# A hybrid decoder block on one core: one weight piece asked for and rounded a step later, retention's tables held in their place, and two probability turns one piece later

## Chip, cores, metric

One core of one Trainium2 chip. The metric is the device time of one execution in microseconds, the median of the runs. Engines: PE (TensorE), DVE (VectorE), ACT (ScalarE), POOL (GpSimd) and SP, which here only issues DMAs.

## The reference

One decoder layer for 1024 rows of width 1024, in float32. What matters here is the part for differential attention:

```
h    = rms_norm(x, norm1_g)
proj = h @ w_in                                  # [1024, 1024] @ [1024, 3584], columns split among the head groups
ret  = rms_norm(retention(rotary(rq), rotary(rk), rv)) * silu(rg)      # 8 heads, chunks of 128 rows
q_d, k_d = rms_norm(dq), rms_norm(dk)            # 4 heads, two score maps each
a    = softmax(q1 k1^T / 8) - lam * softmax(q2 k2^T / 8)               # causal
dif  = rms_norm(a @ v) * (1 - lambda_init)
x    = x + concat([ret, dif]) @ w_out
x    = x + (silu(rms_norm(x) @ w_gate) * (rms_norm(x) @ w_up)) @ w_down
```

## The kernel before, in words

**Products in three parts.** Every large product is done with operands split into a high and a low half (`whi`, `wlo`, and `act` for the rows): three matmuls hi·hi, hi·lo, lo·hi (`mm3`). A weight piece is loaded by SP into `raw`, ACT rounds it (`whi`), DVE takes the rest (`wlo`).

**Steps.** The input projection is done in steps `s` (the loop near L978). Step `s` computes one tile of 128 rows for one column group: eight pieces `k` = 0..7, each one `mm3`. Groups 0 to 3 are the four heads of differential attention (32 steps, 384 columns each), groups 4 to 7 are pairs of retention heads (512 columns). `run` (L509) issues piece `k` and then every operation that is listed for that `k`. Operations of differential attention come from the table `DIF_PLAN` (L76): an entry is (lag, k, function, argument); in step `s` the function works on unit `s - lag`. Unit `u` is row tile `t = u % 8` of head `u // 8`, and its scores have `t + 1` blocks of 128 columns. So a step works on four units at once: it prepares the queries of unit `s-1`, does scores and exponentials of unit `s-2`, and turns and multiplies the probabilities of unit `s-3`.

**The names that follow.** In the order of one step before the change:
- after k = 2 and k = 3 the scores of the two maps (`d_scores`, PE writes `big`); DVE masks them and takes the maximum (`nm`), ACT takes the exponential (`p<-big,nm`);
- after k = 3 the **turn** (`d_turn`, L760): up to four blocks of probabilities of unit `s-3` are transposed by PE (`m<-cs,p`), and after them blocks 4 to 7 in a second turn; after k = 4 ACT **copies** the first four out of PSUM (`d_take`, `aT<-m`), after k = 5 DVE the others;
- after k = 6 the **query turn** (`d_qkturn`, `m<-cs,qkn`) of unit `s-1`, and behind it the **values** product of unit `s-3` (`m<-v,aT`);
- then ACT writes `q` and `kh`, DVE their low halves `q`, `kl` and two casts into `kh`, then the weights `p<-p,by` of unit `s-2`; DVE sums squares of the next unit (`ss`), POOL makes `ms` and `rs` of it, and DVE multiplies (`qkn`), which is what the next query turn reads.

In the first steps the rows of `x` are brought in as well: loaded by SP (`x_load`, `p<-in_x`), transposed by PE in two halves (`x_turn`, **input turn**, also `m<-cs,p`), cast by ACT and subtracted by DVE (`x_split`, `act<-m`), and squared by ACT for the mean (`x_mean`, **square**, `sqx<-p`). Input turns, turns, query turns and values share two PSUM banks (`m`), each free again when its last reader is done.

**Group 1's weight.** `ready` (L954) says in which step each piece of the next group is rounded: piece `k` of group `g` in step `8(g-1) + k`, by `w_part`, once after k = 5 (ACT) and once after k = 6 (DVE). `w_load` asks for the pieces of step `s+1` at the start of step `s`, into two buffers `raw` (NRAW = 2).

**Order.** With `Pinned` (L369) compute operations of the steps keep the order in which the program issues them; others are placed by the scheduler. `r_tables` (L804), three DVE operations that make retention's tables from the row means `ms`, is called at step 32 and is not pinned. `small_loads` (L615) loads gains and lambdas in step 0; `gains` (L627) scales them on DVE in step 1.

Of the kernel before, what the change touches and what calls it, by code (L numbers as in the profile page):

```python
# [20 lines left out]
KC = D // P  # L21
# [31 lines left out]
def constants():  # L53
# [20 lines left out]


DIF_PLAN = [  # L76
    (3, 3, "d_turn", 0),
    (3, 4, "d_take", 0),
    (2, 3, "d_scores", 1),
    (-3, 3, "x_load"),  # L80
    (2, 2, "d_scores", 0),
    (1, 1, "d_sq"),
    (3, 3, "d_turn", 4),
    (-2, 3, "x_turn", 1),
    (3, 5, "d_take", 4),
    (2, 3, "d_max", 0),
# [31 lines left out]
W_PLAN = (5, 6)  # L118
# [245 lines left out]
def block_kernel(ctx: ExitStack, tc: tile.TileContext, x, norm1_g, w_in, ret_norm_g, dq_g, dk_g,  # L364
                 lq1, lk1, lq2, lk2, subln_g, w_out, norm2_g, w_gate, w_up, w_down, cst, out):
    nc = tc.nc
    order = {"pinned": False}
# [131 lines left out]
    def proj(g, t):  # L499

        width = 384 if g < NDH else 512
        pr = prs[g, t] = bankp()
        h = hT[t // 2][:, t % 2]
        for k in range(KC):
            wh, wl = W[g][k]
            mm3(pr[:, :width], h[:, 0, k, :], h[:, 1, k, :], wh, wl, k == 0, k == KC - 1)
            yield

    def run(ops, main):  # L509

        order["pinned"] = main is not None
        for k in range(KC):
            if main is not None:
                next(main)
            for at, f, *args in ops:
                if at == k:
                    f(*args)
        order["pinned"] = False

    def place(plan, names, s, n):  # L520

        return [(at, names[f], s - lag, *args) for lag, at, f, *args in plan if 0 <= s - lag < n]
# [281 lines left out]
    def r_tables():  # L804
        V.reciprocal(rms, ms)
        for dst, at, by in ((vdec, C_VDEC, rms), (eps2, C_EPS, ms)):
            V.tensor_tensor(out=dst, in0=cs[:, at:at + NRH].unsqueeze(1).broadcast_to([P, NT, NRH]),
                            in1=by.unsqueeze(2).broadcast_to([P, NT, NRH]), op=ALU.mult)
# [120 lines left out]
    def o_proj(t, dh):  # L929
        pr = prs["o", t, dh] = bankp()  # L930
        m_ = mT[t // 2][:, t % 2]
        for k in range(KC):
            wh, wl = W[NG + dh][k]
            mm3(pr, m_[:, 0, k, :], m_[:, 1, k, :], wh, wl, k == 0, k == KC - 1)
            yield
# [19 lines left out]
    for g in range(1, NG + 1):  # L955
        for k in range(KC):
            s = (g - 1) * NT + k
            if g == NDH + 1:
                s = max(s, (g - 1) * NT + 4 + k // 2)
            ready.setdefault(s, []).append((g, k, "wp" if g % 2 == 0 else "wd" if g < NDH else "wr"))  # L960
# [17 lines left out]
    for s in range(ND + NR + 3):  # L978
        if s == ND:
            difw.close()  # L980
            rp = ret.enter_context(tc.tile_pool(name="ret", bufs=2, side="right"))
            rg_t = [rp.tile([P, P], F32, name=f"rg{i}", bufs=1) for i in range(2)]
            for i in range(2):
                G.memset(rg_t[i], 0.0)
            qbd_t = [rp.tile([P, 2, P], F32, name=f"qbd{i}", bufs=1) for i in range(2)]
            for qbd in qbd_t:
                G.memset(qbd, 0.0)
            r_tables()
        if s == ND + 2:
            difps.close()  # L990
            rps = retps.enter_context(tc.tile_pool(name="retps", bufs=1, space=bass.MemoryType.PSUM))
        if s == ND + 3:
            dif.close()
            rowb = ctx.enter_context(tc.tile_pool(name="rowb", bufs=NT))
            mixr = [rowb.tile([P, 512], F32, tag="rowb", name="rowb") for _ in range(NT)]
            pools["wr"] = ctx.enter_context(tc.tile_pool(name="wr", bufs=1))
            xp = rets.enter_context(tc.tile_pool(name="xp", bufs=6))
        ops = place(DIF_PLAN, names, s, ND) + place(RET_PLAN, names, s - ND, NR)
        if s == 0:
            ops = [(at, start, what) for at, what in BEGIN] + [op for op in ops if op[1] not in (x_turn, x_split)]  # L1000
            ops += [(7, small_loads)]
        elif s == 1:
            ops += [(5, gains), (7, lambdas)]
            ops += [(at, f, 2, *args) for at, f, *args in LATE]
        ops += [(0, w_load, s + 1)] + [(k, w_part, s) for k in W_PLAN]
        t = s - ND - NR
        if t >= 0:
            ops += [(0, o_load, t, 0), (KC - 1, o_add, t, 0)]
        if s == ND + NR + 2:
            ops += [(3, o_load, 0, 1)]  # L1010
        run(sorted(ops, key=lambda op: op[0]), proj(*divmod(s, NT)) if t < 0 else o_proj(t, 0))
# [299 lines left out]
    for f0 in range(0, NF, 2):  # L1311
        g = Strassen(w_gate, f0, rowb, "rowb").whole() if f0 else firsts[0].out
# [83 lines left out]
```

## Time and profile before

| | |
|---|---|
| median of 3 runs | 1221.82 us (1220.80 to 1221.99) |
| the profiled execution | 1223.85 us, of which the instructions span 1222.0 us |
| PE busy | 1205.5 us, 99% of the span |
| DVE, POOL, ACT busy | 834.7, 571.1, 536.7 us |
| steps of differential attention | about 1.4 to 258 us of the span |

The span runs from the first to the last instruction; 1.85 us of the execution lie around it. PE's busy time is that of matmuls whose ends are modelled, so that a short wait of PE shows less idle time in a row than it costs; the distance between two starts tells more.

### The profile page before, as it was taken

To read this page: it belongs to the slowest core of one execution; us is meant where nothing else is said; L and a number is where in the kernel's file an instruction comes from. 1 tells how busy PE (TensorE), PEld (TensorE's weight loads), DVE (VectorE), ACT (ScalarE), POOL (GpSimd) and SP (SyncE) were. 2 spreads that over 40 slices of the span, in tenths; PEclk is the share of its full clock that TensorE was granted. 3 is DMA by queue.
4 is the path that set the end of the run, shared out by engine and by line. 5 is a ranking of instruction groups with operands and counts; after the bars stand their busy time and mean duration, and the time that the engine had idled before them with its cause. 6 is when DMAs were issued, how large, how long until landed. Compare 5 with 4: busy or idle time off the path is not lost.

```text
span 1222.0 us, 17360 instructions
## 1 busy us (share of the span) xinstructions
PE 1205.5 (99%) x5968; PEld 1024.6 (84%) x5968; DVE 834.7 (68%) x1491; ACT 536.7 (44%) x1194; POOL 571.1 (47%) x719
## 2 busy tenths in 40 slices
PE   8999999999999999999999999999999999999998
PEld 6899989888888888788888888888888888888887
DVE  5988888864444445546988656666566659698697
ACT  6866666653222224334534343333433334444442
POOL 2655555544444443102256456544565436154053
PEclk9999999999999999999899999999999999999999
DMA  6201011103111110422223333323333268943332
GB/s 201 63 26 33 27 29 35 36 10 104 44 44 35 44 35 27 164 87 80 76 87 117 107 106 120 106 87 101 111 114 112 68 226 283 366 142 96 95 117 82
DMA packets 97383, 117.34 MB, mean 96 GB/s; under 512 B 8976, under 2 KB 60304, under 8 KB 97296
## 3 DMA queue, kind: packets, MB, share of 16 engines
q1 hardware_dynamic: 95968, 115.65, 29.4%
q8 instruction: 47, 0.77, 0.3%
q10 hardware_dynamic: 1328, 0.60, 0.2%
q14 instruction: 40, 0.33, 0.1%
HBM read 87.64 MB, written 28.57 MB: 95 GB/s over the span
## 4 chain that ended last, share of the span: by engine, by line
PE 93%; DVE 3%; DMA 2%; issue 1%; ACT 1%; POOL 0%; SPq 0%; ACTq 0%; DVEq 0%; POOLq 0%
PE pp L377 43%; PE h L377 27%; PE m L377 18%; PE big L377 3%; PE o L377 2%; PE it L377 1%; DMA wide<-in_w_down_dram 1%; DMA raw<-in_w_in_dram 1%; DVE act L377 0%; DMA x2d<-x 0%; DVE wlo L377 0%; DVE q L377 0%; DVE x L377 0%; SPq L1295 0%; DVE acc L377 0%
## 5 line engine op out<-in xcount | busy, mean ns | idle before, releaser
L377 PE MATMUL pp<-whi,act 128*128 128x384 f32 (+1 forms) x896 | 287.5, 373 | 0.8 <-ACT whi L377 0.8
L377 POOL TENSOR_TENSOR sum<-rawp 128x512 f32<-128x512 f32 x110 | 157.6, 1434 | 175.5 <-DVE wlo L377 166.4
L377 ACT CAST whi<-sum 128x512 fp32r<-128x512 f32 x165 | 102.6, 622 | 208.0 <-POOL sum L377 66.5
L377 DVE TENSOR_TENSOR wlo<-sum,whi 128x512 fp32r<-128x512 f32 x165 | 165.0, 1001 | 38.6 <-ACT whi L377 38.3
L377 PE MATMUL h<-act,whi 128*128 128x512 f32 x608 | 189.0, 392 | 0.0
L377 PEld LDWEIGHTS pp<-whi,act 128*128 128x128 f32 x896 | 167.3, 189 | 15.3 <-ACT whi L377 1.0
L377 PE MATMUL pp<-wlo,act 128*128 128x384 f32 (+1 forms) x448 | 161.6, 361 | 0.6 <-DVE wlo L377 0.6
L377 POOL TENSOR_TENSOR sum<-wide 128x512 f32<-128x512 f32 x55 | 86.0, 1564 | 129.0 <-DVE wlo L377 111.6
L377 PEld LDWEIGHTS h<-act,whi 128*128 128x128 f32 x608 | 115.2, 190 | 24.0
L377 PE MATMUL pp<-wrh,act 128*128 128x512 f32 x384 | 131.1, 402 | 0.0
L377 PE MATMUL h<-act,wlo 128*128 128x512 f32 x304 | 119.2, 392 | 0.0
L377 PE MATMUL m<-act,whi 128*128 128x512 f32 (+2 forms) x320 | 98.3, 388 | 2.2 <-DVE act L377 2.2
L377 DVE TENSOR_TENSOR wlo<-wide,whi 128x512 fp32r<-128x512 f32 x99 | 77.8, 809 | 32.3 <-ACT whi L377 32.3
L377 PE MATMUL pp<-act,whi 128*128 128x512 f32 (+2 forms) x320 | 98.1, 388 | 0.0
L377 ACT CAST whi<-wide 128x512 fp32r<-128x512 f32 x99 | 59.3, 621 | 83.0 <-PE m L377 43.2
L377 PEld LDWEIGHTS pp<-wlo,act 128*128 128x128 f32 x448 | 85.0, 190 | 7.7 <-DVE wlo L377 1.2
L377 PEld LDWEIGHTS pp<-wrh,act 128*128 128x128 f32 x384 | 72.2, 188 | 14.4
L377 POOL TENSOR_TENSOR fsum<-c 128x512 f32<-128x512 f32 x55 | 78.5, 1438 | 9.9 <-DMA ffd<-fsum 9.9
L377 DVE TENSOR_TENSOR c<-c,h 128x512 f32<-128x512 f32 x86 | 56.8, 682 | 31.2 <-PE h L377 31.1
L377 DVE TENSOR_TENSOR wlo<-rawp,whi 128x512 fp32r<-128x512 f32 x44 | 47.1, 1073 | 40.8 <-ACT whi L377 40.0
L377 PE MATMUL pp<-wrl,act 128*128 128x512 f32 x192 | 74.8, 390 | 0.0
L377 PEld LDWEIGHTS m<-act,whi 128*128 128x128 f32 x320 | 60.5, 191 | 14.2 <-DVE act L377 2.4
(162 smaller groups left out, 2520.6 us busy)
## 6 DMA issues: line engine op xcount, KB each, us to landing
wide<-ffd SPq DMA_DIRECT2D x77, 256.0 KB, 2.7
ffd<-fsum SPq DMA_DIRECT2D x55, 256.0 KB, 2.0
rawp<-in_w_gate_dram SPq DMA_DIRECT2D x22, 512.0 KB, 3.8
rawp<-in_w_up_dram SPq DMA_DIRECT2D x22, 512.0 KB, 3.8
wide<-in_w_down_dram SPq DMA_DIRECT2D x44, 256.0 KB, 5.4
raw<-in_w_in_dram SPq DMA_DIRECT2D x32, 256.0 KB, 2.8
ffd<-c SPq DMA_DIRECT2D x22, 256.0 KB, 2.0
raw<-in_w_in_dram SPq DMA_DIRECT2D x26, 192.0 KB, 2.5
```

Source lines behind the costliest of these rows:

```text
L377: i = getattr(self.engine, op)(*args, **kw)
```

## The change

1. Piece 0 of group 1 is rounded in step 1 in place of step 0, beside piece 1. Both are asked for at the start of step 0. The load of the next piece, which was asked for at the start of step 1, is asked for after k = 7 of that step.
2. `r_tables` is pinned, so its three DVE operations stay at step 32.
3. Both turns (`d_turn` 0 and 4) come after k = 4 in place of k = 3.

```diff
 DIF_PLAN = [
-    (3, 3, "d_turn", 0),
+    (3, 4, "d_turn", 0),
     (3, 4, "d_take", 0),
     (2, 3, "d_scores", 1),
...
     (1, 1, "d_sq"),
-    (3, 3, "d_turn", 4),
+    (3, 4, "d_turn", 4),
     (-2, 3, "x_turn", 1),
...
             s = (g - 1) * NT + k
+            if g == 1:
+                s = max(s, 1)
...
+            order["pinned"] = True
             r_tables()
+            order["pinned"] = False
...
-        ops += [(0, w_load, s + 1)] + [(k, w_part, s) for k in W_PLAN]
+        ops += [(KC - 1 if s == 1 else 0, w_load, s + 1)] + [(k, w_part, s) for k in W_PLAN]
```

On ACT in steps 0 and 1, where `act<-m` are input casts, `whi<-raw` the rounding of a piece of group 1 and `sqx` a square (rows with - are those before, with + those of the change):

```order
 L377 CAST act<-m 128x512
 L377 ACTIVATE sqx,ss<-p 128x1024
-L377 CAST act<-m 128x512
-L377 ACTIVATE whi<-raw,g1col 128x384
-L377 CAST act<-m 128x512
+L377 CAST act<-m 128x512 x2
 L377 ACTIVATE sq<-pp 128x256
 L377 ACTIVATE v<-pp,rs 128x128
```

The rounding that stood between two input casts of step 0 is gone from there; it stands in step 1 ahead of `q`, as the first of two. On SP the third piece of group 1 goes behind the loads of row tiles 4 and 5.

On PE in the step whose probabilities have five blocks (`big` are the two maps' scores, `m<-cs,p` the turns), before and then in the change:

```order
L377 MATMUL big<-kh,q 128x512
L377 MATMUL big<-kl,qz_186 128x512
L377 MATMUL big<-kh,q 128x256
L377 MATMUL big<-kl,qz_186 128x256
L377 MATMUL pp<-whi,act 128x384
L377 MATMUL pp<-wlo,act 128x384
L377 MATMUL pp<-whi,act 128x384
L377 MATMUL m<-cs,p 128x128 x4
L377 MATMUL big<-kh,q 128x512
```

```order
L377 MATMUL big<-kh,q 128x512
L377 MATMUL big<-kl,qz_186 128x512
L377 MATMUL big<-kh,q 128x256
L377 MATMUL big<-kl,qz_186 128x256
L377 MATMUL pp<-whi,act 128x384
L377 MATMUL pp<-wlo,act 128x384
L377 MATMUL pp<-whi,act 128x384
L377 MATMUL m<-cs,p 128x128 x5
L377 MATMUL pp<-whi,act 128x384
```

Before, the first turn stood ahead of the second map's scores and the second turn behind them. Now the scores follow piece 3 at once, piece 4 follows them, and both turns stand together between piece 4 and piece 5.

On ACT in step 3, with what each instruction waits for (`sqx` is the square, `aT` the copy, `act<-m` the input cast, `p<-big` the first exponential), before and then in the change:

```order
L377 ACTIVATE sqx,ss<-p 128x1024 [waits DMAHW5_49,PE_49]
L377 COPY aT<-m 128x128
L377 CAST act<-m 128x512 [waits PE_49]
L377 ACTIVATE p,ls<-big,nm 128x256 [waits DVE_49,Activation_49]
L377 ACTIVATE whi<-raw,g1col 128x384 [waits DMAHW6_49]
```

```order
L377 ACTIVATE sqx,ss<-p 128x1024 [waits PE_49]
L377 COPY aT<-m 128x128
L377 CAST act<-m 128x512
L377 ACTIVATE p,ls<-big,nm 128x256 [waits DVE_49,Activation_49]
L377 ACTIVATE whi<-raw,g1col 128x384 [waits DMAHW6_49]
```

The order on ACT is the same. The copy has no wait of its own in either: the square's wait for PE covers the turn. In the change the input cast has none either, since its input turn now comes ahead of the turn on PE.

## Rows read from the trace of the kernel before

**Rows 1.** The page's first part: busy time of each engine, its share of the span and its instructions.

```profile
PE 1205.5 (99%) x5968; PEld 1024.6 (84%) x5968; DVE 834.7 (68%) x1491; ACT 536.7 (44%) x1194; POOL 571.1 (47%) x719
```

**Rows 2.** Stretches of the span: from and to, length, then busy time of PE, PEld, DVE, ACT, POOL with instructions, the granted clock of PE, the DMA share and GB/s. The first holds steps 0 to 2, the second the eight steps of head 1.

```profile
14.00:32.00 18.00, 15.20 (x88) 13.97 (x87) 11.70 (x32) 11.69 (x31) 7.08 (x17) 0.91 0.42 126
83.00:141.00 58.00, 57.50 (x364) 53.62 (x364) 48.84 (x125) 35.74 (x105) 32.11 (x64) 1.00 0.10 28
```

**Rows 3.** Instructions of ACT in order of time at the end of step 0: start, length, operation, and in brackets the idle time before and what ended it.

```profile
14.35 0.57 ACT L377 CAST act<-m 128x512 fp32r<-128x512 f32 x1
16.27 0.61 ACT L377 ACTIVATE whi<-raw,g1col 128x384 fp32r<-128x384 f32 x1 [1.36 <-DMA raw<-in_w_in_dram]
16.79 0.57 ACT L377 CAST act<-m 128x512 fp32r<-128x512 f32 x1
```

**Rows 4.** Instructions of PE in order of time in steps 1 and 2: three input turns, the query turn of step 1, the first input turn of step 2, the query turn of step 2.

```profile
14.32 0.60 PE L377 MATMUL m<-cs,p 128*128 128x128 f32 x4
...
15.69 0.55 PE L377 MATMUL m<-cs,p 128*128 128x128 f32 x3 [0.25 <-DVE act L377]
...
18.19 0.66 PE L377 MATMUL m<-cs,p 128*128 128x128 f32 x4 [1.85 <-DVE act L377]
...
23.32 0.38 PE L377 MATMUL m<-cs,qkn 128*128 128x128 f32 x2
...
25.13 0.38 PE L377 MATMUL m<-cs,p 128*128 128x128 f32 x2
...
30.02 0.41 PE L377 MATMUL m<-cs,qkn 128*128 128x128 f32 x2 [0.71 <-DVE qkn L377]
```

**Rows 5.** Two stretches, columns as in rows 2.

```profile
18.20:22.50 4.30, 4.30 (x19) 4.20 (x20) 2.37 (x5) 2.88 (x6) 2.29 (x5) 0.60 0.58 160
500.00:520.00 20.00, 18.60 (x95) 15.29 (x94) 9.37 (x15) 7.50 (x18) 2.19 (x7) 1.00 0.53 177
```

**Rows 6.** Step 1: three instructions of DVE in order of time; the issue of the last small load by SP and, from the view of the tile gout, the time from issue to landing of its two loads; the issue of row tile 4 and, from the view of the tile p for this load alone, its time to landing.

```profile
22.73 0.21 DVE L377 TENSOR_SCALAR gout<-gout 128x4 f32<-128x4 f32 x2
22.86 0.61 DVE L377 SCALAR_TENSOR_TENSOR wlo<-raw,g1col,whi 128x384 fp32r<-128x384 f32 x1
24.61 0.35 DVE L377 SCALAR_TENSOR_TENSOR q<-m,gq,q 64x128 fp32r<-64x128 f32 x1 [1.14 <-ACT kh L377]
...
17.68 0.50 SPq L622 DMA_DIRECT2D gout<-in_diff_subln_g_dram  x1
DMA to landing us min/median/max: 4.0/4.2/4.3
...
18.77 0.43 SPq L536 DMA_DIRECT2D p<-in_x_dram  x1
DMA to landing us min/median/max: 4.7/4.7/4.7
```

**Rows 7.** Step 3 in order of time, engine by engine: PE's turn, query turn and values; ACT's square, input cast and q; DVE's subtraction for that input cast; and the square of step 4.

```profile
34.14 0.30 PE L377 MATMUL m<-cs,p 128*128 128x128 f32 x1
37.04 0.38 PE L377 MATMUL m<-cs,qkn 128*128 128x128 f32 x2
37.26 0.27 PE L377 MATMUL m<-v,aT 128*128 128x128 f32 x1
...
34.47 1.06 ACT L377 ACTIVATE sqx<-p 128x1024 f32<-128x1024 f32 x1 [1.40 <-PE m L377]
35.68 0.59 ACT L377 CAST act<-m 128x512 fp32r<-128x512 f32 x1
37.46 0.47 ACT L377 ACTIVATE q<-m,gq 128x256 fp32r<-128x256 f32 x1 [0.23 <-PE m L377]
...
36.30 0.69 DVE L377 TENSOR_TENSOR act<-m,act 128x512 fp32r<-128x512 f32 x1
...
41.52 1.06 ACT L377 ACTIVATE sqx<-p 128x1024 f32<-128x1024 f32 x1 [1.17 <-PE m L377]
```

**Rows 8.** Step 7: the first of the three table operations on DVE, and PE's query turn.

```profile
65.04 0.20 DVE L377 RECIPROCAL rms<-ms 128x8 f32<-128x8 f32 x1 [1.75 <-POOL ms L377]
...
66.54 0.41 PE L377 MATMUL m<-cs,qkn 128*128 128x128 f32 x2 [0.59 <-DVE vdec L377]
```

**Rows 9.** Steps 17 and 18: ACT's copy, first exponential of eight blocks and q; then PE's last matmul ahead of the next turn, that turn and the next query turn; DVE's qkn that this query turn reads.

```profile
138.81 0.59 ACT L377 COPY aT<-m 128x512 f32<-128x512 f32 x1 [2.33 <-PE m L377]
139.47 1.11 ACT L377 ACTIVATE p<-big,nm 128x1024 f32<-128x1024 f32 x1
141.91 0.47 ACT L377 ACTIVATE q<-m,gq 128x256 fp32r<-128x256 f32 x1 [0.72 <-PE m L377]
...
145.89 0.34 PE L377 MATMUL pp<-whi,act 128*128 128x384 f32 x1
146.29 0.41 PE L377 MATMUL m<-cs,p 128*128 128x128 f32 x2
148.96 0.27 PE L377 MATMUL m<-cs,qkn 128*128 128x128 f32 x1
...
148.15 0.42 DVE L377 TENSOR_TENSOR qkn<-pp,rs 128x256 f32<-128x256 f32 x1 [1.14 <-POOL rs L377]
```

**Rows 10.** Step 12: DVE's qkn, and PE's query turn that reads it.

```profile
103.57 0.43 DVE L377 TENSOR_TENSOR qkn<-pp,rs 128x256 f32<-128x256 f32 x1 [0.79 <-POOL rs L377]
...
104.14 0.30 PE L377 MATMUL m<-cs,qkn 128*128 128x128 f32 x1
```

## The prediction

> **What bounds the kernel.** I read the busy times first: TensorE is busy 1205.5 of 1222.0 us [rows 1]. The change adds and removes no instruction of weight, so it can only win or lose where TensorE waits. The table of stretches says where that is: 15.2 us busy of 18 in steps 0 to 2, and 57.5 of 58 in a head further on [rows 2]. Nearly all the rest of the 16.5 idle us lies in stages that the change doesn't touch. Short waits cost more than a row's idle time, because matmul ends are modelled: a turn follows a projection matmul 0.175 us after that one's start where nothing waits, and in step 18 the two starts are 145.89 and 146.29 [rows 9], so this wait costs 0.23. I price waits by starts in that way throughout.
>
> The second thing to see is a loop. A query turn on PE releases ACT (q, kh), then DVE (q, kl, casts, weights p, ss), then POOL (ms, rs), then DVE (qkn), and qkn releases the next query turn. Each step lasts as long as the longer of this loop and PE's own work. A wait of PE that is taken away in a step bound by the loop comes back ahead of the query turn.
>
> **Part 1, the weight piece.** In step 0 ACT stands 1.36 us at the rounding of a piece that has not landed; the input cast behind it starts at 16.79 [rows 3], though its input turn, from 14.32, was done at 14.92. Its bank is wanted by the input turn at 18.19, idle 1.85 [rows 4]. Without the rounding the cast runs at 14.96 (ACT's previous cast, 14.35, is through), DVE's subtraction, 0.69 long as all of them, ends at 16.25, and the input turn goes at 16.3: 1.9 us earlier. After the stall the granted clock is 0.60 over 18.20 to 22.50 [rows 5], so part of it was spent at 1.2 in place of 2.4 GHz; matmuls 0.17 apart stood 0.32 apart there, and I count 1.6 us for it. So PE's query turn of step 1 could move from 23.32 to 19.8, 3.5 us.
>
> Most of that is not kept. DVE's first half of q at 24.61 is what the loop needs, and on DVE two scalings of gout stand ahead of it [rows 6]. They read two small loads; the last is issued at 17.68 and takes 4.0 to 4.3 us [rows 6], so it lands at 21.7 to 22.0, and SP issues it where it did. At present DVE comes to it at 22.73 and nothing waits; in the change DVE would come at about 19.8 and stands. Then two roundings follow in place of one, 0.54 from start to start each: 21.80 + 1.08 = 22.9 for q, 1.7 earlier than 24.61. The loop behind it is unchanged, so the query turn of step 2 moves from 30.02 to 28.3. Row tile 4, ahead of the third piece in the queue now, is issued at 18.3 and lands 4.7 later at most [rows 6], 23.0, where its input turn (25.13 [rows 4]) would want it at 21.6: PE stands 1.4 us there, covered by the same loop (PE has 0.87 in hand at 30.02). The third piece lands some 1.3 us after its old time and is rounded at about 26: covered. **Gain 1.7**; bounds 0.5 (gout at 22.0, plus the clock, below) and 3.5.
>
> **Part 2, the tables.** The scheduler had put the first table operation into step 7, where DVE stands 1.75 us at it for the last row mean, with the maximum and qkn behind it; PE's query turn then starts at 66.54 with 0.59 idle, by starts 0.75 [rows 8]. Held at step 32 its inputs are long there. The three operations, about 0.2 us each, delay ss of step 32 by 0.4 at most; estimated from the rows there, the query turn has over 1 us in hand. **Gain 0.75**, and 0.30 of a turn's wait in the next step, since that turn's weights come sooner.
>
> **Part 3, the turns.** What they gain: a turn now comes later than its weights by piece 4 (0.52) and the second scores (0.2 to 0.9), so none of the waits of turns (0.02 to 0.30, most in steps with few blocks) should be left. The matmuls themselves cost the same in the new order. What they cost lies on ACT, which takes its work in order: the copy now waits for the later turn, and the first exponential, the rounding and q stand behind the copy.
>
> In steps 3 to 5, which also turn row tiles, this is worst. In step 3 the square waits 1.40 for the turn, and the input cast is behind the square [rows 7]. The input cast's own input turn no longer waits for a bank (0.46 gained), but the turn moves from 34.14 to about 35.07 (second scores 0.23, input turn 0.36, piece 4 0.61, less the waits), the square with it, the cast 1.21 after the square's start, DVE's subtraction to 37.9. Its bank is that of the values product, which moves from 37.26 to 37.96: PE loses 0.7. In step 4 the square waits for the turn again (1.17 [rows 7]); the turn comes 1.85 after its old time (0.7 brought along, 0.36 + 0.36 + 0.61 added, 0.18 of its wait gone), and the values product with it: 1.15 more. In step 5 the square waits for DVE and only the copy for the turn: 0.4 more by the same working. In step 6 DVE is 0.2 behind PE and 0.24 of a turn's wait goes. Together these steps **lose 2.25**; bounds 0.7 (step 3 alone) and 3.4 (1.15 each).
>
> In the heads after that I worked through one step that is bound tightly. In step 17 the copy moves from 138.81 to 140.25 (second scores 0.92, piece 4 0.52), and the exponential from 139.47 to 140.73. ACT's 0.72 of idle time ahead of q [rows 9] and 0.1 of overlap take up most of this 1.26; q starts 0.45 later, and the whole loop with it. The next turn's wait (0.23, above) goes, but qkn, done at 148.57, left the query turn at 148.96 only 0.24 in hand [rows 9]. So that turn starts at 148.96 + 0.45 - 0.24 = 149.17, 0.2 later than before. Of the other waits of turns, those at two and three blocks (0.29 each) stand in steps bound by the loop: in step 12 the query turn at 104.14 itself waits 0.16 for qkn, done at 104.00 [rows 10]. They gain nothing. At four blocks 0.15 is gained; at five the later q costs 0.1; from six on PE has more in hand than q loses. A head **loses 0.1**, three heads 0.3. Bounds: -1.0 each, if ACT has room enough, and +1.0 each.
>
> **Sum.** -1.7 - 0.75 - 0.3 + 2.25 + 0.3 = -0.2 us against an execution of 1223.85 us (span 1222.0). The median before stands 2.0 below that execution, so I forecast 1221.82 - 0.2, **1221.6 us**: no difference that can be told. A measurement of this kernel tells about 0.2% from no change, 2.4 us, so faster means below 1219.4 and slower above 1224.3.
>
> On the clock, one rule stands against part 1. The rows: after 0.25 and 1.85 idle the granted clock fell, after 1.4 idle near 512 it stayed at 1.00 [rows 5]. The Trainium skill, "TensorE: Matmul & The Clock Gate", section "What's actually happening", says that the clock follows how busy TensorE has been of late, and that the same kernel can warm up sooner or later from run to run. By that rule the new gap of 1.4 us ahead of row tile 4 may bring the slow clock back, and the sum would be -0.2 + 0.7 = +0.5; by the rows it stays away.
>
> **Rivals.**
> *The waits go and stay away* (faster). The tables, the turns of head 0 (1.1), those of three heads (0.97 each), the banks of input turns (0.7) and 1.7 at the start make 7.2: 1214.6. For it speaks that ACT is the least busy engine [rows 1]; against it, that the square and the cast stand behind the turn on ACT, and the 0.16 and 0.24 in hand in the loop. Chance 0.12.
> *The later copy makes the loop the bound* (slower). This is the mechanism of step 17 in all steps with four blocks of exponentials or more. It decides where q's delay passes what PE has in hand: 0.24 in the step of rows 9, and by the same working 0.3, 0.44, 0.75 and 1.1 in a head's others. At 0.45 it loses next to nothing; at 0.9 it would lose 0.66 + 0.6 + 0.46 + 0.15 = 1.9 a head, 5.6 for three, and the sum is 1226.9 with the terms before it as they are. ACT's idle time ahead of q [rows 9] speaks against it. Chance 0.07.
> *The start doesn't win* (the change doesn't do what it says). DVE's stand at gout is longer, or PE spends the gap and what follows at the lower clock: 4.3 us of work then takes 1.6 more, of which 0.87 is covered. Gain 0 to 1: 1222.3 to 1223.3. Chance 0.13.
>
> **Numbers.** My forecast has 0.68. Its own bounds, with terms that don't all err to one side, are about 1219 to 1223.5; the third rival reaches 1223.3. The range 1219.0 to 1223.8 leaves out the other two rivals, 0.19. Faster: the first rival and a little of the forecast's lower end, 0.15. Slower: the second, 0.07. Same: 0.78.
>
> **What would show it.** Right: ACT's cast at about 15.0 and no half clock at 19 to 22; DVE idle ahead of gout until 21.7; the query turn of step 2 near 28.3; in steps 3 and 4 PE idle ahead of the values product for about 0.9 each, behind an input cast's subtraction; no table operation in step 7; q of step 17 following its rounding without idle time; the end of the 32nd step within 1 us of where it was. Wrong: values products of steps 3 to 5 that don't wait (then faster), idle time ahead of most query turns (then slower), or DVE passing gout before 21.7.

## The result, and the profile after

| | before | after |
|---|---|---|
| median of 16 runs each | 1221.58 us | 1224.22 us (1222.22 to 1227.65) |
| ratio of the times, 95% interval | | 1.0031 (1.0023 to 1.0040): 3.8 us slower (2.8 to 4.9) |
| profiled execution, its span | 1223.85, 1222.0 us | 1223.91, 1222.1 us |

The forecast was 1221.6 with a range up to 1223.8 and "no difference". The change is slower. (The two medians as they stand differ by 2.6; I go by the ratio.)

The two profiled executions are equally long, and that misleads: 592.55 us into the span of before, and 594.91 into that of after, PE ends the same wait of 2.16; after is 2.36 late there. But then before's execution went on at half clock for 10.24 us and after's for 6.83, in work that the change doesn't touch. So I compare where the same instruction stands, up to step 30:

| query turn of step | 1 | 2 | 3 | 6 | 7 | 8 | 9 | 30 |
|---|---|---|---|---|---|---|---|---|
| before | 23.32 | 30.02 | 37.04 | 58.48 | 66.54 | 74.81 | 83.18 | 234.43 |
| after, less before | -3.46 | -0.35 | -0.90 | +1.71 | +1.02 | +0.62 | +0.64 | +1.98 |

The 3.5 us won by step 1 are nearly gone at step 2. From the query turn of step 3 to that of step 6 the change loses 2.6, by step 8 it has gained 1.1 back, and the heads lose 1.4 more. The rows that answer to [rows 4], PE at the start:

```profile
17.85 0.60 PE L377 MATMUL m<-cs,p 128*128 128x128 f32 x4
...
19.86 0.38 PE L377 MATMUL m<-cs,qkn 128*128 128x128 f32 x2
...
23.69 0.63 PE L377 MATMUL m<-cs,p 128*128 128x128 f32 x4 [1.85 <-DMA p<-in_x_dram]
...
25.05 0.34 PE L377 MATMUL big<-kh,q 128*128 128x128 f32 x1 [0.21 <-DVE kh L377]
...
29.67 0.38 PE L377 MATMUL m<-cs,qkn 128*128 128x128 f32 x2
```

The stall of 1.85 ahead of an input turn is not gone: it has moved from 18.19 to 23.69, to row tile 4, which now is not there. To [rows 3, 6] answer these: ACT's casts without the rounding between them (two in one row), DVE's stand at gout, and row tile 4's issue and time to landing:

```profile
14.30 1.23 ACT L377 CAST act<-m 128x512 fp32r<-128x512 f32 x2
...
22.10 0.35 DVE L377 TENSOR_SCALAR gout<-gout 128x4 f32<-128x4 f32 x2 [2.20 <-DMA gout<-in_ret_norm_g_dram]
22.38 1.15 DVE L377 SCALAR_TENSOR_TENSOR wlo<-raw,g1col,whi 128x384 fp32r<-128x384 f32 x2
23.55 0.71 DVE L377 SCALAR_TENSOR_TENSOR q<-m,gq,q 64x128 fp32r<-64x128 f32 x2
...
18.29 0.84 SPq L536 DMA_DIRECT2D p<-in_x_dram  x2
...
DMA to landing us min/median/max: 5.3/5.3/5.3
```

Two stretches, columns as in [rows 2]. The first shows the clock: half (1.2 GHz) behind the new stall, where [rows 5] show it behind the old one. The second is head 1, where PE was busy 57.50.

```profile
25.20:28.50 3.30, 3.30 (x14) 3.30 (x15) 2.53 (x9) 2.66 (x8) 1.38 (x3) 0.50 0.18 52
83.00:141.00 58.00, 56.99 (x361) 53.56 (x360) 48.79 (x123) 34.47 (x104) 32.31 (x64) 1.00 0.10 28
```

Step 3 to [rows 7] (PE's turn, query turn and values; ACT's square and cast; DVE's subtraction), and the values products of steps 4 and 5:

```profile
34.48 0.27 PE L377 MATMUL m<-cs,p 128*128 128x128 f32 x1
36.14 0.44 PE L377 MATMUL m<-cs,qkn 128*128 128x128 f32 x2 [0.32 <-ACT aT L377]
37.35 0.49 PE L377 MATMUL m<-v,aT 128*128 128x128 f32 x2 [0.78 <-DVE act L377]
...
34.78 1.06 ACT L377 ACTIVATE sqx<-p 128x1024 f32<-128x1024 f32 x1 [2.08 <-PE m L377]
...
35.98 0.59 ACT L377 CAST act<-m 128x512 fp32r<-128x512 f32 x1
...
36.60 0.69 DVE L377 TENSOR_TENSOR act<-m,act 128x512 fp32r<-128x512 f32 x1 [0.93 <-PE m L377]
...
45.53 0.71 PE L377 MATMUL m<-v,aT 128*128 128x128 f32 x4 [0.78 <-DVE act L377]
...
53.34 0.82 PE L377 MATMUL m<-v,aT 128*128 128x128 f32 x5 [0.51 <-DVE act L377]
```

The square follows the later turn, the cast the square, the subtraction the cast, and the values product waits for the bank. Step 7 to [rows 8] has no table operation and no wait of the query turn:

```profile
65.44 0.96 DVE L377 TENSOR_REDUCE nm<-big 128x1 f32<-128x768 f32 x1
66.88 0.42 DVE L377 TENSOR_TENSOR qkn<-pp,rs 128x256 f32<-128x256 f32 x1 [0.48 <-POOL rs L377]
...
67.56 0.44 PE L377 MATMUL m<-cs,qkn 128*128 128x128 f32 x2
```

Steps 17 and 18 to [rows 9]: q has no idle time ahead of it, and the query turn of step 18 now waits for qkn.

```profile
141.74 1.12 ACT L377 ACTIVATE p<-big,nm 128x1024 f32<-128x1024 f32 x1
...
143.34 0.47 ACT L377 ACTIVATE q<-m,gq 128x256 fp32r<-128x256 f32 x1
...
150.14 0.41 PE L377 MATMUL m<-cs,qkn 128*128 128x128 f32 x2 [0.25 <-DVE qkn L377]
```

### The profile page after: what moved, and what is told of

Same layout as the page of the kernel before. It is cut to its first block, busy times and chain, and to the rows that moved or that the text cites. A ratio compares the mean times of both kernels' runs of the same rounds, so it can differ in the third digit from the quotient of the medians.

```text
span 1222.1 us, 17369 instructions
## 1 busy us (share of the span) xinstructions
PE 1203.0 (98%) x5968; PEld 1024.7 (84%) x5968; DVE 836.8 (68%) x1491; ACT 533.3 (44%) x1194; POOL 570.5 (47%) x719
## 4 chain that ended last, share of the span: by engine, by line
PE 89%; DVE 4%; ACT 2%; POOL 2%; issue 1%; DMA 1%; SPq 0%; ACTq 0%; DVEq 0%; POOLq 0%
PE pp L377 40%; PE h L377 27%; PE m L377 18%; PE big L377 2%; PE o L377 2%; PE it L377 1%; POOL rs L377 1%; DMA raw<-in_w_in_dram 1%; DVE p L377 1%; ACT p L377 0%; DVE act L377 0%; DVE q L377 0%; DMA x2d<-x 0%; DMA gout<-in_diff_subln_g_dram 0%; DVE qkn L377 0%
## 5 line engine op out<-in xcount | busy, mean ns | idle before, releaser
L377 PE MATMUL pp<-whi,act 128*128 128x384 f32 (+1 forms) x896 | 293.4, 375 | 0.8 <-ACT whi L377 0.8
```

Of the source, the lines that this page charges most:

```text
L377: i = getattr(self.engine, op)(*args, **kw)
```

## The experiments

Ratios are to runs of before on the same chip, with 95% intervals; 0.001 is 1.2 us. "Step 2" is the start of that step's query turn.

### The parts one by one

Part 1 alone (`ready` and `w_load` as in the change).

> Part 1 alone (the weight piece a step later; turns and tables as before). Theory A (row tile 4 lands at 23.6, PE stands 1.85 and its clock falls to half again, so that part 1 wins little): PE idle 1.8 to 1.9 ahead of the first input turn of step 2, half clock for some 3.4 us behind it, query turn of step 2 at 29.5 to 29.8 (30.02 before), of step 3 near 36.1, of step 30 at 233.5 to 234.1 (234.43 before). Rival B (the start wins the 1.7 of the prediction and the rest of the change took it away again): query turn of step 2 at 28.3, of step 30 near 232.7, the time 1.7 us under before. Rival C (the late load hurts later steps): query turn of step 30 at 235 or later.

Measured: 1222.91, ratio 1.0010 (0.9999 to 1.0021). PE stood 2.61 ahead of row tile 4, whose load landed at 24.86; half clock followed at 25.61:

```profile
25.00 0.63 PE L377 MATMUL m<-cs,p 128*128 128x128 f32 x4 [2.61 <-DVE wlo L377]
...
30.67 0.38 PE L377 MATMUL m<-cs,qkn 128*128 128x128 f32 x2
```

The row names DVE's low halves of the weight pieces (`wlo`), which end at 24.93, 0.07 after the landing; that the turn waits for the tile and not for them is shown by the run with the row sooner (below), where it goes at 22.04, before they begin. Rival B falls. Step 30 came 0.68 later than in before's profile, so theory A's "a little earlier" was missed too: part 1 does not win little, it wins nothing. Step 30 at 235.11 is what rival C asked for, but from step 2 on it takes 204.44, against 204.41 in before: the late load doesn't hurt later steps.

Part 2 alone (`r_tables` pinned).

> Part 2 alone (tables kept at step 32). Theory A: no wait of DVE for the last row mean in step 7, the query turn of that step (66.54 before) 0.75 earlier, of the next step 1.0 earlier, and of step 30 (234.43) still 0.7 to 1.0 earlier; the time 0.7 to 1.0 us lower, which cannot be told from none by the runs alone. Rival B (it comes back ahead of the next query turns, since those steps are bound by the loop): query turn of step 30 within 0.2 of 234.43.

Measured: 1220.49, ratio 0.9998 (0.9984 to 1.0011). Against before's profile the query turns of steps 6, 8 and 30 stand -1.74, -2.93 and -2.90: 1.2 gained between steps 6 and 8, and kept. Theory A by the rows, with 0.2 more than it said; by the ratio, 0.2 us, no gain can be told. The -1.74 are there from step 1 on, and they are the finding that matters. PE at the start, DVE at gout, and the stretch of [rows 5]:

```profile
18.04 0.66 PE L377 MATMUL m<-cs,p 128*128 128x128 f32 x4 [1.84 <-DVE act L377]
...
21.60 0.38 PE L377 MATMUL m<-cs,qkn 128*128 128x128 f32 x2
...
28.29 0.41 PE L377 MATMUL m<-cs,qkn 128*128 128x128 f32 x2 [0.68 <-DVE qkn L377]
...
21.55 0.22 DVE L377 TENSOR_SCALAR gout<-gout 128x4 f32<-128x4 f32 x2
...
18.20:22.50 4.30, 4.30 (x29) 4.23 (x29) 3.18 (x9) 3.14 (x8) 2.29 (x5) 1.00 0.61 173
```

The start is that of before, with the same stall of 1.84, and the clock did not fall. Step 2 is at 28.29, which is what the prediction gave for the change with part 1 (28.3). DVE comes to gout at 21.55, 0.08 after the last of its loads landed (21.47): where the clock stays up, the old start already runs into the bound that I had set for the new one.

Part 3 in steps 3 to 6 alone, and from step 7 on alone. The edit, in the second with `s >= 7`:

```diff
+OLD_PLAN = [(3, 3, *e[2:]) if e[2] == "d_turn" else e for e in DIF_PLAN]
...
-        ops = place(DIF_PLAN, names, s, ND) + ...
+        ops = place(DIF_PLAN if s < 7 else OLD_PLAN, names, s, ND) + ...
```

> Part 3 in steps 3 to 6 alone (later steps turn as before; piece and tables as before). Theory A (on ACT the square and the input cast stand behind the later turn, and values waits for that cast's bank): the query turn of step 6 (58.48 before) 2.0 to 2.7 later, PE idle 0.5 to 0.8 ahead of the values products of steps 3, 4 and 5, step 30 (234.43) 2.0 to 2.7 later, the time 2 to 3 us above before. Rival B (the loss of after in these steps comes from the start, which brought the later rows in later, and not from the turns): query turn of step 6 within 0.5 of 58.48, and the time the same as before.

Measured: 1223.67, ratio 1.0021 (1.0009 to 1.0033). From step 2 to step 6 it loses 2.28, to step 8 2.81, with the waits of 0.78, 0.78 and 0.50 ahead of the values products. Theory A. (The 0.5 between steps 6 and 8 is not in the whole change, which takes 15.24 there, against 15.14 with the tables alone.)

> Part 3 from step 7 on alone (steps 3 to 6 turn as before; piece and tables as before). Theory A (q later by 0.4 costs more than the prediction's 0.1 a head): between the query turns of step 7 (66.54) and of step 30 (234.43) 1.0 to 1.6 us more than before, 0.3 to 0.45 a head, in the steps with five blocks and more, PE idle ahead of query turns for qkn; the time 1.0 to 1.6 us above before. Rival B (the prediction's size, the rest of the loss belongs to the tables or the start): 0.1 a head, 0.2 to 0.5 in all. Rival C (without the other parts the waits of turns are simply saved): step 30 earlier than 234.43.

Measured: 1222.04, ratio 1.0009 (0.9997 to 1.0022). Between steps 9 and 30 it loses 1.18, some 0.4 a head, and at the same places in each: 0.18 between steps 9 and 10, 0.25 between 10 and 11, 0.10 between 14 and 15, and 0.14 gained between 13 and 14. A head is of theory A's size; from step 7, where theory A started, it is only 0.81 in all, below its 1.0, since step 7 itself came 0.38 late and that was gone by step 8. Step 10, DVE and PE:

```profile
89.21 0.42 DVE L378 TENSOR_TENSOR qkn<-pp,rs 128x256 f32<-128x256 f32 x1 [1.14 <-POOL rs L378]
89.55 0.68 DVE L378 COPY aT<-m 128x512 f32<-128x512 f32 x1
...
89.78 0.41 PE L378 MATMUL m<-cs,qkn 128*128 128x128 f32 x2 [0.25 <-DVE qkn L378]
```

### The start: which wait it is

gout's loads and scalings out of the way, with part 1 alone ("..." marks what is left out here):

```diff
+    def gout_loads():
         nc.sync.dma_start(gout[:, 0:4], ...)
         nc.sync.dma_start(gout[:, 4:5], ...)
...
+    def gains_out():
         V.tensor_scalar_mul(gout[:, 0:4], gout[:, 0:4], HD ** 0.5)
         V.tensor_scalar_mul(gout[:, 4:5], gout[:, 4:5], 1.0 - LAMBDA_INIT)
...
+        elif s == 2:
+            ops += [(7, gout_loads)]
+        elif s == 4:
+            ops += [(7, gains_out)]
```

> Part 1 alone, with gout's two loads moved behind step 2 and its two scalings into step 4, so that DVE has no small load of these ahead of q; row tile 4 stays in its place. Theory A (row tile 4's landing bounds the start, not DVE's stand at gout): PE still stands ahead of the first input turn of step 2 until that tile is down, some 1 to 2.5 us, half clock behind it, query turn of step 2 at 28.3 or later. Rival B (DVE's stand at gout is what holds it): DVE's first half of q near 21.1, query turn of step 2 near 26.5 (21.1 + the 5.4 it took in before), the time 1 to 3 us under part 1 alone (1222.9).

Measured: 1219.05, ratio 0.9983 (0.9971 to 0.9994): by the ratios 3.3 us under part 1 alone, with an uncertainty of some 2. With gout's two issues gone from ahead of it, row tile 4 landed at 22.42 and PE did not stand:

```profile
21.43 1.14 DVE L377 SCALAR_TENSOR_TENSOR wlo<-raw,g1col,whi 128x384 fp32r<-128x384 f32 x2
22.76 0.71 DVE L377 SCALAR_TENSOR_TENSOR q<-m,gq,q 64x128 fp32r<-64x128 f32 x2 [0.19 <-ACT kh L377]
...
28.15 0.41 PE L377 MATMUL m<-cs,qkn 128*128 128x128 f32 x2 [0.71 <-DVE qkn L377]
```

Rival B by the time, if not by its q of 21.1 (the clock had fallen at 9.41 here); theory A's stand is missing. That fall also brought PE to the input turn later (query turn of step 1 at 21.47, against 19.86 in the change), so this execution can't show that a tile at 22.42 costs nothing. And the edit moved the tile's landing, so the next run moved the tile alone: `load_x(4)` ahead of the lambdas' loads, gout as in the change.

> Part 1 alone with row tile 4 asked for ahead of the lambdas' loads (gout and its scalings in step 1, as in the change). Theory A (row tile 4's landing is what PE stood for, and that stand brings the half clock): no wait of PE ahead of the first input turn of step 2 and no half clock near 25; DVE still stands at gout until its loads are down, 21.5 to 23.5, so the query turn of step 2 is at 28 to 29.5 with PE idle 1 to 2.5 ahead of it, and the time 0.5 to 1.5 us above part 1 with gout later (1219.05). Rival B (gout alone was the trouble): the same time as part 1 alone, 1222.9, and idle time of 2 us and more ahead of the query turn of step 2 with a half clock behind it. Rival C (gout costs nothing once the row tile is there): query turn of step 2 below 27.5 and the time as with gout later.

Measured: 1223.67, ratio 1.0019 (1.0009 to 1.0029), by the ratios 1.1 us above part 1 alone, which is within the uncertainty. Rival B: with the tile down at 18.47, DVE still stood at gout, PE then at the scores behind it, and half clock followed at 26.02; step 2 is at 30.17.

```profile
22.59 0.37 DVE L377 TENSOR_SCALAR gout<-gout 128x4 f32<-128x4 f32 x2 [2.33 <-DMA gout<-in_ret_norm_g_dram]
...
25.56 0.30 PE L377 MATMUL big<-kh,q 128*128 128x128 f32 x1 [2.39 <-DVE kh L377]
```

So gout on DVE is enough by itself to take the gain; whether the late row tile alone would be, no run shows. Parts 1 and 2 with both loads mended, and both loads moved with part 2 alone:

> Parts 1 and 2, gout later as in the run before this one, and row tile 4 asked for ahead of the lambdas' loads, four issues sooner; turns as before the change. Theory A (the late landings ate part 1's gain): row tile 4 down by 20, no wait of PE ahead of its input turn, no half clock near 25, query turn of step 1 at 19.9 and of step 2 at 26.2 to 27 (28.3 with tables alone, where the clock did not fall), of step 30 at 229.5 to 231 (231.5 with tables alone, 234.4 before); the time 1 to 2 us under tables alone (1220.5), about 1219. Rival B (something else waits next, the third piece, lambdas or row tile 5): query turn of step 2 or 3 late again, step 30 at 231.5 or later, the time as tables alone. Rival C (it is the weight piece in step 1 itself that costs): as part 1 alone, 1222 to 1223.

Measured: 1218.46, ratio 0.9983 (0.9970 to 0.9995). Step 1 at 21.21 and step 2 at 27.89, later than theory A, since here the clock had fallen at 9.19; step 30 at 231.16. PE no longer stands long at the start: 0.43 ahead of an input turn, 0.68 ahead of the query turn of step 2, for the loop. The step from part 2 alone, 1.8 us by the ratios, is within the intervals.

> Part 2 and the two moved loads (row tile 4 sooner, gout later), with the weight piece where it was before the change: ACT still stands at its rounding in step 0. Theory A: the stall of 1.8 us ahead of the input turn of step 0 stays, so the query turn of step 1 stays at 21.6 to 23.3; step 30 as with tables alone, 231.5 (or 233.5 where the clock falls at 19), the time as tables alone, 1220 to 1221. Rival B (the loads' order is worth something by itself): the time 1 us or more under that.

Measured: 1219.81, ratio 0.9992 (0.9981 to 1.0003). The stall of 1.81 stays, step 2 is at 28.35 and step 30 at 231.63: theory A.

> The whole change with the two moved loads (row tile 4 sooner, gout later). Theory A: the start as in the mended start, the turns cost what they cost in the runs with them alone (2.3 to 2.8 in steps 3 to 6, 1.0 to 1.3 after), so step 30 is 3.3 to 4.1 us later than in the mended start and the time 3 to 4 us above it, about 1222.5. Rival B (what steps 3 to 5 lose comes from rows that land late): with row tile 4 sooner the waits of 0.5 to 0.8 ahead of values in steps 3 to 5 are gone, and it is within 1.5 of the mended start.

Measured: 1220.62, ratio 1.0000 (0.9989 to 1.0012), 2.1 us above the mended start, where 3 to 4 were expected, with an uncertainty of some 2. The trace is plainer: from step 2 to step 30 it takes 206.66 in place of 203.27, 3.4 more, with waits ahead of values of 0.78, 0.78 and 0.50. Theory A, not rival B. Against the change itself the two moved loads give back 3.8 us.

> Parts 1 and 2 as in the change, turns as before it. Theory A (part 1 loses by itself): PE idle 1.5 to 2.7 ahead of the first input turn of step 2, half clock near 25 for 3.4 us, query turn of step 2 at 29.5 to 30.8, of step 30 at 233 to 234.5; the time 0.3 to 1.2 us under part 1 alone (1222.9), 2 to 3 us under the whole change. Rival B (the start is a matter of luck, and part 1 alone drew badly): no half clock near 25 and query turn of step 2 at 28.5 or sooner.

Measured: 1220.94, ratio 0.9998 (0.9986 to 1.0009). PE stood 2.24 ahead of row tile 4 and half clock followed at 25.22, here for 6.83 us; step 2 at 31.14: theory A, a little late. By the ratios it is 1.5 us under part 1 alone and 4.0 under the whole change. Rival B falls: behind such a stand the clock fell in all four executions that have one.

### Steps 3 to 5: the order on ACT

```diff
     (1, 4, "d_qkn"),
+    (-2, 3, "x_split", 1),
     (0, 3, "x_mean"),
...
-    (-2, 4, "x_split", 1),
     (2, 7, "d_weights"),
```

> The whole change with the two moved loads, and the second input cast and its subtraction (x_split 1) put after k = 3, ahead of the square and the copy on ACT. Theory A (in steps 3 to 5 values waits because that cast stands behind the square, whose buffer the later turn frees): the waits of 0.78, 0.78 and 0.50 ahead of the values products are gone, from the query turn of step 2 to that of step 6 it takes 28.5 to 29.3 in place of 30.73, and the time is 1.5 to 2.2 us under the change with the moved loads (1220.6). Rival B (the copies and q behind the square set the step, and the values' wait only stands for them): PE idle ahead of the query turns instead, the time within 0.5 of 1220.6.

Measured: 1221.34, ratio 1.0000 (0.9989 to 1.0010). From step 2 to step 6 it takes 28.91 in place of 30.73, without a wait ahead of values: theory A on the mechanism. Its time was missed: both ratios are 1.0000, with an uncertainty of some 2 us. The same move in step 1 puts a subtraction ahead of what the query turn of step 2 needs, which costs 0.75 between steps 1 and 2 (7.44 in place of 6.69, here and in the next run), and the clock had fallen at 9.60 in this execution.

> The mended start (parts 1 and 2, two moved loads, turns as before), with the second input cast after k = 3 as in the run before this one. Theory A (with the turns at their old place the bank is free in time, but for 0.46 of an input turn's wait in step 3): 0 to 0.7 us under the mended start (1218.5), query turns of step 2 to step 6 28.0 to 28.6 apart (28.57 in the mended start). Rival B (the subtraction now ahead of qkn on DVE lengthens the loop): 0.4 a step later in steps 2 to 5, the time 1 to 2 us above the mended start.

Measured: 1223.19, ratio 1.0013 (1.0001 to 1.0025), by the ratios 3.7 us above the mended start. With the turns in their old place the same move loses 2.5 from step 2 to step 6, more than rival B said: the subtraction stands ahead of qkn on DVE, and the query turn waits.

```profile
41.66 0.69 DVE L377 TENSOR_TENSOR act<-m,act 128x512 fp32r<-128x512 f32 x1 [0.57 <-ACT act L377]
42.26 0.41 DVE L377 TENSOR_TENSOR qkn<-pp,rs 128x256 f32<-128x256 f32 x1
...
42.82 0.41 PE L377 MATMUL m<-cs,qkn 128*128 128x128 f32 x2 [0.26 <-DVE qkn L377]
```

### The heads

From step 7 on the first turn stands after k = 4, the second stays after k = 3.

> From step 7 on only the first turn (blocks 0 to 3) after k = 4; the second (blocks 4 to 7) stays after k = 3, before it. Piece, tables and steps 3 to 6 as before the change. Theory A (two losses a head: ACT's later copy delays q, 0.18 between the query turns of steps 9 and 10, and DVE's later copy of blocks 4 to 7 delays the values product and DVE's half of q, 0.25 between those of steps 10 and 11): no wait of the values product for that copy in steps 10, 18 and 26, the distance of the query turns of steps 10 and 11 back at 6.94 to 7.0 (6.94 before, 7.19 with both late), that of steps 9 and 10 still 7.65 to 7.75 (7.53 before, 7.71 with both late). Rival B (all of it is ACT's copy, which a later q carries into the step after): 7.15 to 7.2 for steps 10 and 11 as with both late.

Measured: 1222.83, ratio 1.0013 (1.0001 to 1.0025). Steps 10 and 11 are 7.13 apart, near rival B; values still waits for DVE's copy. The distance of steps 9 and 10 rose to 8.09, because the second turn, now the first to come, waits 0.66 for the weights, so the run isn't a clean test.

> The mended start (parts 1 and 2, two moved loads), and the turns after k = 4 only in the steps that turn four blocks (steps 14, 22, 30). Theory A (there the turn's wait of 0.29 is on the path): the distance of the query turns of steps 13 and 14 is 6.95 (7.09 before), likewise in the next head, no other distance moves by over 0.05; the time within 0.5 of the mended start (1218.5), which the runs alone can't tell. Rival B (the neighbours pay for it): the next distance (7.34 before) longer by 0.1 or more.

Measured: 1218.49, ratio 0.9976 (0.9967 to 0.9985). Rival B: steps 13 and 14 are 6.94 apart (0.15 gained), the next 7.75 (0.41 lost), since the turn of step 15, in its old place, waits for weights that the loop now brings later against PE. Its lead on before is put down to the mended start, which it contains; in this execution the clock did not fall, and step 2 is at 26.41.

## Why the prediction was wrong

**The start, the step that failed.** "Gain 1.7" was a difference to one execution. Its 1.6 for the clock are real: the way from the stalled input turn to the query turn of step 1 takes 5.13 in [rows 4] and 3.56 at full clock with tables alone. But they were not the change's to win. In six profiled executions with the old start and its stall of 1.8 the clock fell in three. ("Turns early" is part 3 in steps 3 to 6 alone, "turns late" from step 7 on alone; PE's stand is its longest wait between 13 us and the scores of step 2, ahead of an input turn or, with the row sooner, ahead of the scores.)

| start | PE's stand | clock fell at | step 2 |
|---|---|---|---|
| before; turns early; first turn late only | 1.85, 1.76, 1.82 | 18.98, 19.02, 18.62 | 30.02, 30.66, 30.24 |
| tables alone; loads moved alone; turns late | 1.84, 1.81, 1.87 | not | 28.29, 28.35, 28.90 |
| the change; part 1; parts 1 and 2; part 1, row sooner | 1.85, 2.61, 2.24, 2.39 | 25.17, 25.61, 25.22, 26.02 | 29.67, 30.67, 31.14, 30.17 |
| gout later; mended; change mended; four blocks only | 0.44, 0.43, 0.24, 0.24 | 9.41, 9.19, not, not | 28.15, 27.89, 27.05, 26.41 |

The falls at 9.41 and 9.19 come before the stands beside them. The two kernels with the cast put first have another order in step 1 and are left out. The means of step 2 are 29.4 for the old start, 30.4 for the change's, 27.4 for the mended one. So part 1 costs 1.0 where I had it gain 1.7; the runs with part 1 alone say 1.2 (-0.1 to 2.6). I counted the fallen clock twice: as before's cost in the sum, and again, in part, by starting from a median 2.0 below the execution that had it. Only in part, because that execution also had the longest stretch of half clock near 590 us; over the whole span its clock was 0.994, against a mean of 0.996 in 128 runs of before.

The clocks of all runs, not of profiled ones alone, point the same way. Worked out from each run's mean clock over the span, which is on record to three digits, a run of before spends 8.9 us at half clock (standard error 0.3), a run of the three kernels that have part 1, gout in step 1 and the turns of before spends 11.1 (0.6; 35 runs, one with a clock of 0.946 left out), and a run of the four in the last line of the table 7.6 (0.5; 48 runs). By this estimate the clock costs part 1 about 1.1 us (0.4) more than it costs before, which is as much as part 1 loses in all. The 16 runs of the change have 9.6 (0.9), which tells nothing by itself.

Two sizes were off as well, and each was again read from one trace. gout's loads landed at 22.07 to 23.68 in the four executions of the change's start, not 21.7 to 22.0; row tile 4, where it stands behind them, took 5.3 to 6.2 from its issue, not 4.7 at most. In the five executions that keep before's loads the last of gout's landed anywhere from 21.47 to 23.25, and row tile 4 took 4.7 to 5.7. So PE stood 1.85 and more, not 1.4, and DVE's q came at 23.55, not 22.9. And "covered by the same loop" failed: the clock, which the sum left at full, fell behind that stand each time, and PE, not the loop, brought the query turn of step 2, which in the change has no wait for qkn (29.67, above; qkn was done at 28.80). The rule of the Trainium skill that the prediction set against this ("TensorE: Matmul & The Clock Gate", "What's actually happening") had the side right. Its remark that the same kernel can warm up sooner or later from run to run fits the runs here, whose clock differs too: the 128 runs of before have mean clocks from 0.994 to 1.000. The rival "the start doesn't win" was this, with too small a price.

**Tables: right.** 1.05 forecast (0.75 and 0.30), 1.2 by the rows; the runs can't tell it from none.

**Steps 3 to 6: right.** 2.25 forecast; 2.3 to step 6 in the run with these turns alone, and 2.2 between the mended start with and without the turns, by the chain foretold. Moving the cast ahead of the square took the values' waits away.

**The heads: right mechanism, wrong size.** 0.1 a head forecast, 0.4 measured. q is later by 0.42 (0.48 after the query turn of step 9 in before, 0.90 with late turns), where I had worked out 0.45, and I let 0.24 "in hand" at the next query turn swallow half. It swallows it for one step only. The terms that I had are there: 0.18 at step 10 for my 0.2, 0.10 at five blocks for 0.1, 0.14 gained at four for 0.15. Missing from the sum is 0.25 at step 11. On DVE qkn stands ahead of the copy, maximum, rounding and q, so the loop also runs from qkn to qkn. In before, the query turn of step 11 (97.66) follows the end of its qkn (97.58) at once. The qkn that the query turns of steps 10 and 11 read, in before and then with late turns (that of step 10 is shown above):

```profile
89.90 0.42 DVE L377 TENSOR_TENSOR qkn<-pp,rs 128x256 f32<-128x256 f32 x1 [1.14 <-POOL rs L377]
97.15 0.43 DVE L377 TENSOR_TENSOR qkn<-pp,rs 128x256 f32<-128x256 f32 x1 [0.97 <-POOL rs L377]
...
96.40 0.42 DVE L378 TENSOR_TENSOR qkn<-pp,rs 128x256 f32<-128x256 f32 x1 [0.92 <-ACT aT L378]
```

They start 7.25 apart in before and 7.19 with late turns, so a later qkn is hardly caught up, and the whole 0.42 comes through, 0.18 at step 10 and 0.25 at step 11. This is argued from the rows; the run meant to test it was not clean.

**Sum.** Start +1.0, tables -1.2, turns +3.4 (from step 2 to step 30, with and without them on the mended start) make 3.2, against 3.8 (2.8 to 4.9) measured. The parts' own ratios add up to 4.6, and parts 1 and 2 in one kernel with part 3's two runs to 3.4, each with some 3 us of uncertainty. What stays open is whether the clock always falls behind the new stand: four executions of four show it, and with the old stall, nearly as long, it fell in three of six. Open, too, is why: stands of 1.81 to 1.87 are in both lots, so their length alone doesn't settle it.

## What to carry to other kernels

A profile is one draw: before a gain is counted from a stretch at half clock, ask whether the median run has that stretch at all, and compare the profile's own time and granted clock with those of the runs. The landing of a load is a draw as well: gout's second load took 3.9 to 5.0 us from its issue in five executions with the same start. Work that is moved earlier runs into whatever small load was hidden by its lateness; look on each in-order engine for the first operation that reads a load, and move that load's user away with it, here 3.3 us, uncertain by some 2, for two scalings and their loads that were wanted only much later. Slack ahead of one engine's instruction is worth nothing if the loop that binds the next step does not pass through that instruction.

## What the runs showed of the hardware

Half-clock stretches away from the span's end were 3.41, 6.83 or 10.24 us long in all sixteen profiled executions. The one behind the wait of 2.16 near 590 us, in work that no kernel here touches, came out at each of the three, which by itself hides parts of this change in a comparison of two profiles. The six small loads at the end of their queue, four of lambdas and two of gout, came down one behind another: where gout's stand there, they landed 0.2 to 0.5 after the last of lambdas', and 3.9 to 5.9 us after their own issue.
